# Norm steps given out beside products, TensorE's order fixed where the feed-forward begins

## The chip, the cores and the metric

The kernel runs on one core of a Trainium2 chip. The metric is the time of one execution on the device, in microseconds (us). Three runs of the kernel before gave 1806.92, 1814.36 and 1819.08 us; the median is 1814.36 us. The engines are named as the profile names them: PE is TensorE (matmul; PEld its weight load), DVE is VectorE, ACT is ScalarE, POOL is GpSimd, SP is SyncE, which issues most DMA transfers.

## The reference

One layer of a streaming encoder, for 1024 prompt frames and 32 sample frames of width 1024, in float32:

```python
h = h + (merged.astype(h.dtype) @ w_out).astype(h.dtype)      # merged: three gated branches
xn2 = rmsnorm(h, norm_ffn)                                     # y = h * rsqrt(mean(h*h) + 1e-6) * g
gu = xn2 @ w_gate_up                                           # 1024 -> 2 x 2816
gate, up = gu[..., :FFN_HIDDEN], gu[..., FFN_HIDDEN:]
h = h + ((jax.nn.silu(gate) * up) @ w_down).astype(h.dtype)    # 2816 -> 1024
y = rmsnorm(h, norm_final)
```

The mixers in front of `merged` (a state space model, spatial gating, stick-breaking attention) take about half of the time and are not touched.

## The kernel before

**Layout and products.** The rows of `h` lie in nine blocks: b = 0 to 7 are 128 prompt rows each, b = 8 the 32 sample rows. Half 0 is blocks 0 to 3, half 1 blocks 4 to 8. A float32 product is made of three matmuls (`mm3`, L144 to L146): each operand is split into a rounded high part (an ACT copy) and a remainder (a subtraction on DVE or POOL).

**The stages that matter.** `gates(half)` makes the merged branches `mt` (a high and a low tile, in eight slices m; for half 1 slice 3 is made last). `out_proj(half)` runs four quarters q of 256 columns; in each it multiplies `mt` of every block with a piece of `w_out` (24 matmuls of 128x256 a block, 16 of 64x256 for block 8) and DVE adds the result to `h`. `norm2(chunk)` then makes the operands of the feed-forward for one half. For each block it takes a sum of squares (ACT), the reciprocal root by bit trick and three Newton steps on one column (`rstd_of`, DVE), the scaled row tile `xb` (DVE), eight transposes of `xb` (PE, L1190), and from two pairs of blocks seven split operands each, by sums and differences of quarters (a Strassen-Winograd form: seven products in place of eight). `xb` has one buffer. `up_tile(i, chunks)` does one of the 22 tiles of 128 hidden columns: it loads two raw weight tiles, makes seven split stationary weights from them (L1244 to L1265: ACT, POOL and DVE), and runs seven products of 12 matmuls a chunk, in the order w1, w2, ws2, ws3, wu, ws1, ws4. Chunk 0 is 256 wide, chunk 1 is 272.

**The order of the program before** is: `gates(0)`, `out_proj(0)`, `gates(1)`, `norm2(0)`, `out_proj(1)`, `norm2(1)`, then a lead of tiles 0 and 1 with chunk 0 and tiles 0 and 1 with chunk 1 (weights are made anew for each of the four), then tiles 2 to 21 with both chunks. The down product reads the activations back from DRAM (`act_d`) in eleven groups of 256 rows (`load_act`: a DMA to `ra`, an ACT copy to `act`, remainders on POOL and DVE) and adds to `h`, which `norm2` stored in `h_d` and which comes back as `hd0` and `hd1`.

**What sets the order.** Every engine works its own instructions in order. A scheduler lays them out from the program's order, their dependencies and the buffers that are free; a DMA that SP issues waits behind the ones that stand before it. Large tiles share slots: pool `hx` and pool `hy` have four slots each, given out in turn; weights go through rings of four `wh`, four `wl` and two `raw` tiles; PSUM has six banks for products (`p`) and two for transposes (`ptn`).

Of the kernel before, what the change touches and what calls it, by code (L numbers as in the profile page):

```python
# [17 lines left out]
T = TP + TS  # L18
# [30 lines left out]
def trunk_kernel(ctx: ExitStack, tc: tile.TileContext,  # L49
# [1027 lines left out]

    def h_rows(b):
        return H[b // 4][:, b % 4, :] if b < 8 else hS


# [60 lines left out]
    def out_proj(half, mt):  # L1142
        wo = w_out[0].rearrange("(k p) c -> p k c", p=128)
        for q in range(4):
            us = tm_units(wo, 256 * q)
            for b, (t0, rows, h, off) in enumerate(BLOCKS):
                if h != half:
                    continue
                d = h_rows(b)[:, 256 * q:256 * q + 256]
                if b == 8:  # L1150
                    ps = ps_any()[0:64, 0:256]
                    tm_sample(ps, mt2, us)
                    tmp = late.tile([32, 512], F32, name="htmp")[:, 0:256]
                    add_pair(tmp, ps, tmp)
                    v.tensor_add(d, d, tmp)
                    continue
                ps = ps_any()[0:rows, 0:256]
                tm_dense(ps, mt, off, rows, us)
                v.tensor_add(d, ps, d)
# [4 lines left out]
    PAIRS = (((0, 2), (1, 3)), ((4, 6), (5, 7)))  # L1164
# [30 lines left out]

    def make_operands(wk, X, o, n, x11, x21, second):

        def split(i, raw, eng):
            hi, lo = X[i][0][:, :, o:o + n], X[i][1][:, :, o:o + n]
            s.activation(hi, raw, AF.Copy)  # L1200
            eng.tensor_sub(lo, raw, hi.bitcast(F32))

        def tmp(name, tag, bufs):
            return wk.tile([128, 4, 128], F32, name=name, tag=tag, bufs=bufs)[:, :, 0:n]

        r11 = tmp("r11", "r11", 1)
        s.activation(r11, x11, AF.Copy)
        split(0, x11, v)
        split(1, x21, v)
        x12, x22 = second()  # L1210
        t1 = tmp("t1", "xt", 2)
        v.tensor_sub(t1, x12, r11)
        split(3, t1, g)
        t2 = tmp("t2", "xt", 2)
        v.tensor_sub(t2, x22, t1)
        split(2, x22, v)
        split(4, t2, g)
        t3 = tmp("t3", "xt", 2)
        v.tensor_sub(t3, t2, r11)
        split(5, t3, g)  # L1220
        v.tensor_sub(r11, x21, t2)
        split(6, r11, g)

    def norm2(chunk, wk, X):
        for j, (ba, bb) in enumerate(PAIRS[chunk]):
            xa = scaled(wk, ba)
# [3 lines left out]
            def second():  # L1230
                xb = scaled(wk, bb)
                return [turned(xb, 128, q, ps_turn()) for q in range(2)]

            make_operands(wk, X, 128 * j, 128, x11, x21, second)
        if chunk:
            xs_ = scaled(wk, 8)
            a0, a1 = turned(xs_, 32, 0, ps_turn()), turned(xs_, 32, 1, ps_any())
            make_operands(wk, X, 256, 16, a0[:, :, 0:16], a1[:, :, 0:16], lambda: (a0[:, :, 16:32], a1[:, :, 16:32]))
        sp.dma_start(h_d[chunk], H[chunk])
# [12 lines left out]
    def up_tile(i, wk, chunks, X):  # L1252
# [12 lines left out]
        ws2, ws3, ws1, ws4 = stationary(g1, g), stationary(u1, v), stationary(u2, g), stationary(g2, g)  # L1265

        def product(w, x):
            out = {}
            for c in chunks:
                ps = out[c] = ps_any()[:, 0:WIDTH[c]]  # L1270
# [47 lines left out]
    with pool("wg", 1) as wk:  # L1318
        mA = gates(0, wk)
        sp.dma_start(gb, dram_bcast(norm_ffn, 1024))  # L1320
        out_proj(0, mA)
        mB = gates(1, wk)
    with pool("wu", 1) as wk:
# [3 lines left out]
        norm2(0, wk, X0)  # L1327
        out_proj(1, mB)
        sm = [big(hy, "xo4"), big(hy, "xo5"), big(hx, "xo6")]
# [124 lines left out]
```

## Time and profile before

| What | us |
|---|---|
| median of three runs | 1814.36 |
| the profiled execution, its own time | 1813.17 |
| its span, first to last instruction | 1811.5 |
| PE busy in the span | 1658.8 (92%) |
| DVE busy | 991.4 (55%) |
| ACT busy | 594.9 (33%) |
| POOL busy | 603.6 (33%) |
| chain that ended last: PE / DVE / issue / POOL | 61% / 15% / 10% / 6% |
| mean granted TensorE clock (1 is 2.4 GHz) | 0.954 |

How to read it: PE carries most of the chain, so time can be won where PE stands still or runs at the lower clock. In the profile's 40 slices PE's busy share falls to 5 tenths in slice 21, to 7 or 8 in its neighbours and again to 7 near slice 34; slices 21 and 23 to 25 are the stretch from the end of `gates(1)` to the first tiles of the feed-forward, and slice 34 is the hand-over to the down product.

### The profile page before, as it was taken

To read this page: it belongs to the slowest core of one execution; us is meant where nothing else is said; L and a number is where in the kernel's file an instruction comes from. 1 tells how busy PE (TensorE), PEld (TensorE's weight loads), DVE (VectorE), ACT (ScalarE), POOL (GpSimd) and SP (SyncE) were. 2 spreads that over 40 slices of the span, in tenths; PEclk is the share of its full clock that TensorE was granted. 3 is DMA by queue.
4 is the path that set the end of the run, shared out by engine and by line. 5 is a ranking of instruction groups with operands and counts; after the bars stand their busy time and mean duration, and the time that the engine had idled before them with its cause. 6 is when DMAs were issued, how large, how long until landed. Compare 5 with 4: busy or idle time off the path is not lost.

```text
span 1811.5 us, 28082 instructions
## 1 busy us (share of the span) xinstructions
PE 1658.8 (92%) x10949; PEld 1507.4 (83%) x10949; DVE 991.4 (55%) x1909; ACT 594.9 (33%) x1082; POOL 603.6 (33%) x363
## 2 busy tenths in 40 slices
PE   7988998999989899999978578999999997999997
PEld 6977896777777788799977578999999997888875
DVE  7952514312799730911285666666555554666645
ACT  5322322223566532212233333333333332212214
POOL 2210211333011233434444244333332334645534
PEclk9998999699999999999988889999999998999999
DMA  7453245256656427754351232322232225333202
GB/s 219 120 133 71 79 140 129 64 157 187 166 138 170 128 79 239 254 176 140 91 193 31 87 108 78 95 75 72 81 91 77 71 71 188 120 95 95 71 26 94
DMA packets 273502, 212.62 MB, mean 117 GB/s; under 512 B 68372, under 2 KB 246584, under 8 KB 272856
## 3 DMA queue, kind: packets, MB, share of 16 engines
q1 hardware_dynamic: 244808, 195.61, 36.7%
q10 hardware_dynamic: 28560, 15.21, 2.8%
q8 instruction: 86, 1.41, 0.3%
q14 instruction: 48, 0.39, 0.1%
HBM read 154.88 MB, written 55.30 MB: 116 GB/s over the span
## 4 chain that ended last, share of the span: by engine, by line
PE 61%; DVE 15%; issue 10%; POOL 6%; DMA 4%; ACT 3%; SPq 1%; POOLq 0%; ACTq 0%; DVEq 0%
PE p L146 13%; PE p L145 13%; PE p L144 13%; DVE om L831 4%; PE p_d L144 3%; PE p_d L146 3%; PE p_d L145 3%; POOL wl L118 3%; PE p_av L144 2%; PE p_av L146 1%; PE p_av L145 1%; DVE rs_m L169 1%; POOL hS L1401 1%; DMA raw<-in_w_gate_up_dram 1%; DVE wtl L862 1%
## 5 line engine op out<-in xcount | busy, mean ns | idle before, releaser
L118 POOL TENSOR_TENSOR wl<-raw,wh 128x1024 fp32r<-128x1024 f32 x120 | 303.1, 2533 | 760.7 <-ACT wh L117 702.9
L117 ACT ACTIVATE wh<-raw 128x1024 fp32r<-128x1024 f32 x120 | 126.4, 1058 | 360.4 <-PE p L146 160.0
L144 PE MATMUL p<-xo,wh 128*128 128x256 f32 (+1 forms) x616 | 177.1, 288 | 3.7 <-ACT wh L1248 1.8
L144 PE MATMUL p<-xo,wl 128*128 128x256 f32 (+1 forms) x616 | 176.9, 287 | 1.1 <-DVE fa L1305 1.1
L146 PE MATMUL p<-xo,wh 128*128 128x256 f32 (+1 forms) x616 | 177.0, 287 | 0.8 <-POOL wh L1249 0.8
L145 PE MATMUL p<-xo,wh 128*128 128x256 f32 (+1 forms) x616 | 177.5, 288 | 0.0
L146 PE MATMUL p<-xo,wl 128*128 128x256 f32 (+1 forms) x616 | 176.4, 286 | 0.9 <-POOL wl L1249 0.9
L145 PE MATMUL p<-xo,wl 128*128 128x256 f32 (+1 forms) x616 | 176.8, 287 | 0.0
L144 PE MATMUL p_d<-xnh,wh 128*128 128x272 f32 (+1 forms) x464 | 158.3, 341 | 10.4 <-ACT vb L377 7.2
L146 PE MATMUL p_d<-xnh,wl 128*128 128x272 f32 (+1 forms) x464 | 155.7, 336 | 5.2 <-POOL wl L118 5.2
L145 PE MATMUL p_d<-xnl,wh 128*128 128x272 f32 (+1 forms) x464 | 155.4, 335 | 0.0
L1407 DVE TENSOR_TENSOR hd<-p,hd 128x512 f32<-128x512 f32 x160 | 106.3, 683 | 65.7 <-PE p L146 65.7
L145 PE MATMUL p<-wl,act 128*128 128x512 f32 x352 | 138.6, 394 | 2.5 <-POOL wl L118 2.5
L146 PE MATMUL p<-wh,act 128*128 128x512 f32 x352 | 138.3, 393 | 0.0
L144 PE MATMUL p<-wh,act 128*128 128x512 f32 x352 | 138.0, 393 | 0.0
L1249 POOL TENSOR_TENSOR wh<-raw,wh 128x512 fp32r<-128x512 f32 x60 | 80.3, 1342 | 153.8 <-ACT wh L1248 153.8
L1249 POOL TENSOR_TENSOR wl<-raw,wl 128x512 fp32r<-128x512 f32 x60 | 79.9, 1334 | 154.4 <-ACT wl L1248 154.3
L144 PEld LDWEIGHTS p<-xo,wh 128*128 128x128 f32 x616 | 118.0, 192 | 4.1 <-ACT wh L1248 2.0
L144 PEld LDWEIGHTS p<-xo,wl 128*128 128x128 f32 x616 | 117.7, 191 | 2.0 <-issue 1.3
L146 PEld LDWEIGHTS p<-xo,wh 128*128 128x128 f32 x616 | 118.1, 192 | 1.1 <-POOL wh L1249 1.1
L146 PEld LDWEIGHTS p<-xo,wl 128*128 128x128 f32 x616 | 117.4, 191 | 1.4 <-POOL wl L1249 1.4
L145 PEld LDWEIGHTS p<-xo,wh 128*128 128x128 f32 x616 | 117.8, 191 | 0.0
(454 smaller groups left out, 4439.7 us busy)
## 6 DMA issues: line engine op xcount, KB each, us to landing
raw<-in_w_in_dram SPq DMA_DIRECT2D x66, 512.0 KB, 3.9
raw<-in_w_gate_up_dram SPq DMA_DIRECT2D x48, 512.0 KB, 4.6
ra<-act_d SPq DMA_DIRECT2D x22, 528.0 KB, 3.6
raw<-in_w_down_dram SPq DMA_DIRECT2D x22, 512.0 KB, 3.7
q<-q_d SPq DMA_DIRECT2D x64, 128.0 KB, 3.0
raw<-in_w_out_dram SPq DMA_DIRECT2D x16, 512.0 KB, 5.9
act_d<-fs SPq DMA_DIRECT2D x44, 128.0 KB, 4.0
act_d<-fa SPq DMA_DIRECT2D x44, 128.0 KB, 4.0
```

The lines of the kernel that those rows point to most:

```text
L117: s.activation(wh, raw, AF.Copy)
L118: g.tensor_sub(wl, raw, wh.bitcast(F32))
L144: pe.matmul(ps, ah, bh, start=start, stop=False)
L145: pe.matmul(ps, ah, bl, start=False, stop=False)
L146: pe.matmul(ps, al, bh, start=False, stop=stop)
L169: v.scalar_tensor_tensor(t, y, mh, y, op0=OP.mult, op1=OP.mult)
L831: v.tensor_tensor_scan(rev, rev, rev, 1.0, op0=OP.mult, op1=OP.bypass)
L862: v.tensor_sub(wl[:, lo:512], pt[:, lo:512], wh[:, lo:512].bitcast(F32))
L1249: eng.tensor_sub(lo, src, hi.bitcast(F32))
L1401: g.tensor_add(hr[:, cs], hr[:, cs], tmp)
L1407: v.tensor_add(hr[:, cs], ps, hr[:, cs])
```

## The change

Five things change, all between `out_proj(0)` and the first group of the down product.

1. The sums of squares move from `norm2` into `out_proj`: after the second and the fourth quarter ACT squares 512 columns of a block into a column of `ss2`. `norm2` adds the two and makes the reciprocal roots of all blocks of a half at once (`rstd_all`, 128x5).
2. The scaled rows `xb` are made by POOL (times the gain `gb`) and ACT (times the root) in place of one DVE instruction.
3. `norm2` becomes a generator. Its steps are given out beside products: `norm2(0)` beside `out_proj(1)` (transposes after every second block), `norm2(1)` beside tiles 0 and 1 of chunk 0 (transposes after every third product). PE's order in this stretch is taken as written (`manual_schedule`).
4. The lead is tile 0 and tile 1 with chunk 0, tile 1 with chunk 1 (its weights are held), tile 0 with chunk 1: three weight preparations in place of four. One remainder of the held tiles moves from DVE to POOL (`light`).
5. In the down product the first `act` takes a slot of `hx`, and `hd0`, `hd1` are allocated after it.

```diff
+    ss2 = late.tile([128, 20], F32, name="ss2")
...
-    def out_proj(half, mt):
+    def out_proj(half, mt, junk, beside=iter(())):
...
+            for b in PAIRS[half][0] + PAIRS[half][1] + ((8,) if half else ()):
+                t0, rows, h, off = BLOCKS[b]
+                next(beside, None)
...
+                if q % 2:
+                    c = slice(256 * q - 256, 256 * q + 256)
+                    s.activation(junk()[0:rows], h_rows(b)[:, c], AF.Square, scale=1.0 / 32,
+                                 accum_out=ss2[0:rows, 10 * half + 5 * (q // 2) + (b % 4 if b < 8 else 4):][:, 0:1])
...
-    def scaled(wk, b):
-        rows = BLOCKS[b][1]
-        xb = wk.tile([128, 1024], F32, name="xb")
-        hr = h_rows(b)
-        ss = wk.tile([128, 1], F32, name="rs_ss", bufs=2)
-        s.activation(xb[0:rows], hr, AF.Square, scale=1.0 / 32, accum_out=ss[0:rows])
-        r = rstd_of(wk, ss[0:rows], rows)
-        v.scalar_tensor_tensor(xb[0:rows], hr, r, gb[0:rows], op0=OP.mult, op1=OP.mult)
-        return xb[0:rows]
+    def rstd_all(wk, ss, n):
+
+        m = wk.tile([128, 20], F32, name="rs_a")
+        mm, y, t = [m[:, 5 * i:5 * i + n] for i in range(3)]
+        v.tensor_scalar(mm, ss, EPS, None, op0=OP.add)
+        v.tensor_scalar(y.bitcast(I32), mm.bitcast(I32), -0.5, 1597463007.0, op0=OP.mult, op1=OP.add)
+        v.tensor_scalar(mm, mm, -0.5, None, op0=OP.mult)
+        for _ in range(3):
+            v.tensor_mul(t, y, y)
+            v.tensor_mul(t, t, mm)
+            v.scalar_tensor_tensor(y, t, 1.5, y, op0=OP.add, op1=OP.mult)
+        return y
...
+    def norm2(chunk, wk, X, gap):
+
+        def scaled(b):
+            i, rows = b % 4 if b < 8 else 4, BLOCKS[b][1]
+            xb = wk.tile([128, 1024], F32, name="xb")[0:rows]
+            g.tensor_mul(xb, h_rows(b), gb[0:rows])
+            s.activation(xb, xb, AF.Copy, scale=r[0:rows, i:i + 1])
+            return xb
...
+        for j in range(2):
+            xa = scaled(order[2 * j])
+            for _ in range(gap):
+                yield
             x11 = turned(xa, 128, 0, ps_turn())
             x21 = turned(xa, 128, 1, ps_any())
...
-        norm2(0, wk, X0)
-        out_proj(1, mB)
...
-        norm2(1, wk, X1)
-        X = (X0, X1)
         NF = FF // 128
-        lead = 2
-        for c in range(2):
-            for i in range(lead):
-                up_tile(i, wk, (c,), X)
-        for i in range(lead, NF):
+        with tc.manual_schedule(engines={mybir.EngineType.PE}):
+            work = norm2(0, wk, X0, 2)
+            out_proj(1, mB, lambda: wk.tile([128, 512], F32, name="junk2", tag="xt", bufs=2), work)
+            for _ in work:
+                pass
...
+            work = norm2(1, wk, X1, 3)
+
+            up_tile(0, wk, (0,), X, up_weights(0, True), work)
+            held = up_weights(1, True)
+            up_tile(1, wk, (0,), X, held, work)
+            for _ in work:
+                pass
+        up_tile(1, wk, (1,), X, held)
+        up_tile(0, wk, (1,), X)
+        for i in range(2, NF):
             up_tile(i, wk, (0, 1), X)
...
-        for half in range(2):
-            H[half] = hx.tile([128, 4, 1024], F32, name=f"hd{half}", tag="hx")
-            sp.dma_start(H[half], h_d[half])
...
-        acts = [load_act(0), load_act(1)]
+        acts = [load_act(0, hx)]
+        for half in range(2):
+            H[half] = hx.tile([128, 4, 1024], F32, name=f"hd{half}", tag="hx")
+            sp.dma_start(H[half], h_d[half])
+        acts.append(load_act(1))
```

**How it moves instructions.** On PE, before the change, the end of `out_proj(1)` (L132 is block 8), all transposes of `norm2(1)` in a row, and the first product (of `xo`, the operands):

```order
L132 MATMUL p_9940<-wh,mt_6925 64x256
L132 MATMUL p_9940<-wl,mt_6925 64x256
L1190 MATMUL ptn<-ident,xb 128x128 x4
L1190 MATMUL p_9983<-ident,xb 128x128 x4
L1190 MATMUL ptn<-ident,xb 128x128 x12
L1190 MATMUL p_10054<-ident,xb 128x128 x4
L1190 MATMUL ptn<-ident,xb 128x128 x8
L1190 MATMUL ptn<-ident,xb 128x32 x4
L1190 MATMUL p_10125<-ident,xb 128x32 x4
L144 MATMUL p_10183<-xo_9266,wh 128x256
```

On PE with the change, the end of the third product of tile 0, chunk 0 (36 matmuls stand before this place since `out_proj(1)`), and the fourth product:

```order
L145 MATMUL p_10053<-xo_9286,wl 128x256
L146 MATMUL p_10053<-xo_9286,wl 128x256
L1202 MATMUL ptn<-ident,xb 128x128 x4
L1202 MATMUL p_10072<-ident,xb 128x128 x4
L144 MATMUL p_10086<-xo_9286,wh 128x256
L145 MATMUL p_10086<-xo_9286,wh 128x256
```

The transposes of each block now stand between products, and PE reaches them in this order whatever else is ready.

On POOL with the change, the piece from the scaling of the third block of half 1 (block 5) to that of block 8 (`xb` is the new product with the gain, `xo` an operand's remainder, `wh` and `wl` remainders of tile 1's weights):

```order
L1213 TENSOR_TENSOR xb<-h_9037,gb 128x1024
L1222 TENSOR_TENSOR xo_9973<-t_10142,xo_9973 128x4x128
L1222 TENSOR_TENSOR xo_9974<-t_10146,xo_9974 128x4x128
L1286 TENSOR_TENSOR wh<-raw,wh 128x512
L1286 TENSOR_TENSOR wl<-raw,wl 128x512
L1213 TENSOR_TENSOR xb<-h_9037,gb 128x1024
L1222 TENSOR_TENSOR xo_9974<-t_10152,xo_9974 128x4x128
L1222 TENSOR_TENSOR xo_9287<-r_10077,xo_9287 128x4x128
L1286 TENSOR_TENSOR wh<-raw,wh 128x512
L1286 TENSOR_TENSOR wl<-raw,wl 128x512
L1213 TENSOR_TENSOR xb<-hS,gb 32x1024
```

Before, POOL had no `xb` in its queue, and the eight large `xo` remainders of half 1 stood in two runs of four with one `wl` between them; now weights, remainders and scalings take turns.

On SP, the hand-over to the down product before the change (`hd0` is issued far ahead of this piece, right behind the weight loads of tile 1):

```order
L116 DMA raw<-in_w_down_dram 128x1024
L1347 DMA hd_15698<-h_d_6928 128x4096
L116 DMA raw<-in_w_down_dram 128x1024
L1313 DMA act_d<-fs 128x256 x2
L1316 DMA act_d<-fs 128x16
L116 DMA raw<-in_w_down_dram 128x1024
L1313 DMA act_d<-fa 128x256
L116 DMA raw<-in_w_down_dram 128x1024
L1313 DMA act_d<-fa 128x256
L1316 DMA act_d<-fa 128x16
L1355 DMA ra<-act_d 128x1056 x10
```

and with the change:

```order
L1355 DMA act_d<-fs 128x256 x2
L1358 DMA act_d<-fs 128x16
L116 DMA raw<-in_w_down_dram 128x1024
L1355 DMA act_d<-fa 128x256 x2
L1358 DMA act_d<-fa 128x16
L116 DMA raw<-in_w_down_dram 128x1024
L1401 DMA ra<-act_d 128x1056 x2
L1467 DMA hd_15650<-h_d_6929 128x4096
L1467 DMA hd_15652<-h_d_6930 128x4096
L1401 DMA ra<-act_d 128x1056 x6
```

The first two `ra` loads stand behind the last store to `act_d` in both; `hd0` and `hd1` have moved behind them.

## Rows read from the trace of the kernel before

**Rows 1.** Busy time by stretch (us): engines with instruction counts, granted clock, DMA share, GB/s.

```profile
935.76:962.17 26.41, 5.53 (x25) 4.76 (x25) 17.99 (x41) 9.66 (x17) 8.32 (x7) 0.55 0.13 40
962.17:1018.72 56.55, 56.55 (x466) 56.31 (x464) 26.48 (x55) 15.28 (x27) 19.77 (x12) 0.97 0.16 52
1018.72:1055.02 36.30, 6.81 (x33) 5.63 (x33) 25.52 (x56) 13.99 (x28) 13.37 (x11) 0.57 0.38 124
1055.02:1104.08 49.06, 45.48 (x338) 44.46 (x338) 31.88 (x55) 19.95 (x42) 22.12 (x19) 0.94 0.30 92
1521.79:1531.36 9.57, 0.01 (x2) 0.01 (x1) 2.53 (x3) 1.51 (x2) 2.54 (x2) 0.70 0.67 226
```

**Rows 2.** PE's waits from 935 to 1125 us: in total, times, longest.

```profile
PE ptn L1190 <- DVE xb L1184: 50.4, 7, 9.7
```

**Rows 3.** Instructions on the tile xb (ns, min/median/max).

```profile
L1184 DVE SCALAR_TENSOR_TENSOR xb<-h,rs_m,gb x8: 1283/1284/1287, 941.6 to 1041.9; 128x1024 f32<-128x1024 f32 x8
```

**Rows 4.** PE's timeline after the first gap: start, duration, line.

```profile
962.95 0.41 PE L144 MATMUL p<-wh,m 128*128 128x256 f32 x1
...
966.01 0.29 PE L144 MATMUL p<-wh,m 128*128 128x256 f32 x1
966.13 0.28 PE L145 MATMUL p<-wl,m 128*128 128x256 f32 x1
...
968.04 1.03 PE L1190 MATMUL ptn<-ident,xb 128*128 128x128 f32 x8
```

**Rows 5.** Timeline of ACT and DVE at the end of gates(1).

```profile
937.16 0.66 ACT L1132 ACTIVATE m<-acc 128x544 fp32r<-128x544 f32 x1 [0.38 <-DVE acc L1131]
...
937.85 2.07 DVE L1133 TENSOR_TENSOR m<-acc,m 128x544 fp32r<-128x544 f32 x1 [0.72 <-ACT m L1132]
```

**Rows 6.** Instructions on the tile xo (the operands), ns.

```profile
L1201 POOL TENSOR_TENSOR xo<-t,xo x15: 322/1270/1312, 952.4 to 1057.1; 128x512 fp32r<-128x512 f32 x12, 128x64 fp32r<-128x64 f32 x3
```

**Rows 7.** Instructions on yf, of line L1249, of line L118 and on hd, ns.

```profile
L1367 POOL TENSOR_TENSOR yf<-hd,gfin x8: 2347/2407/2411, 1759.3 to 1803.5; 128x1024 f32<-128x1024 f32 x8
L1370 ACT ACTIVATE yf<-yf,rs_m x8: 1132/1138/1153, 1764.0 to 1803.5; 128x1024 f32<-128x1024 f32 x7, 32x1024 f32<-32x1024 f32 x1
...
L1249 POOL TENSOR_TENSOR wl<-raw,wl x60: 1264/1294/1743, 1011.1 to 1499.0; 128x512 fp32r<-128x512 f32 x60
...
L118 POOL TENSOR_TENSOR wl<-raw,wh x120: 2339/2398/5723, 9.3 to 1751.3; 128x1024 fp32r<-128x1024 f32 x120
...
L1410 ACT ACTIVATE junk<-hd x16: 614/631/634, 1755.2 to 1804.5; 128x512 f32<-128x512 f32 x16
```

**Rows 8.** DVE's timeline in the root's Newton steps, and a remainder beside POOL.

```profile
957.02 1.19 DVE L170 SCALAR_TENSOR_TENSOR rs_m<-rs_m 128x1 f32<-128x1 f32 x1
...
958.50 0.16 DVE L170 SCALAR_TENSOR_TENSOR rs_m<-rs_m 128x1 f32<-128x1 f32 x1
...
1065.06 1.46 DVE L1249 TENSOR_TENSOR wl<-raw,wl 128x512 fp32r<-128x512 f32 x1
```

**Rows 9.** PE's timeline in tile 2: its waits in brackets.

```profile
1111.37 0.35 PE L144 MATMUL p<-xo,wl 128*128 128x256 f32 x1 [1.06 <-DVE fa L1305]
...
1120.76 0.39 PE L144 MATMUL p<-xo,wh 128*128 128x272 f32 x1 [1.83 <-DVE fs L1288]
```

**Rows 10.** Timeline at the hand-over to the down product.

```profile
1043.29 0.34 SPq L1347 DMA_DIRECT2D hd<-h_d  x1
...
1507.16 0.38 SPq L1347 DMA_DIRECT2D hd<-h_d  x1
...
1525.25 0.42 SPq L1316 DMA_DIRECT2D act_d<-fa  x1
1525.73 0.96 SPq L1355 DMA_DIRECT2D ra<-act_d  x2
1529.99 1.08 ACT L1356 ACTIVATE act<-ra 128x1056 fp32r<-128x1056 f32 x1 [7.26 <-DMA ra<-act_d]
...
1538.62 0.69 DVE L1407 TENSOR_TENSOR hd<-p,hd 128x512 f32<-128x512 f32 x1 [2.54 <-PE p L146]
```

More of the change, by code (lines that the diff above doesn't have):

```diff
@@ L1230, in second, with both @@
             def second():
-                xb = scaled(wk, bb)
+                xb = scaled(order[2 * j + 1])
+                for _ in range(gap):
+                    yield
                 return [turned(xb, 128, q, ps_turn()) for q in range(2)]
-            make_operands(wk, X, 128 * j, 128, x11, x21, second)
+            yield from operands_of(128 * j, 128, x11, x21, second)
         if chunk:
-            xs_ = scaled(wk, 8)
+            xs_ = scaled(8)
+            sp.dma_start(h_d[chunk], H[chunk])
+            for _ in range(gap):
+                yield
             a0, a1 = turned(xs_, 32, 0, ps_turn()), turned(xs_, 32, 1, ps_any())
-            make_operands(wk, X, 256, 16, a0[:, :, 0:16], a1[:, :, 0:16], lambda: (a0[:, :, 16:32], a1[:, :, 16:32]))
-        sp.dma_start(h_d[chunk], H[chunk])
+            def both():
+                yield
+                return a0[:, :, 16:32], a1[:, :, 16:32]
+            yield from operands_of(256, 16, a0[:, :, 0:16], a1[:, :, 0:16], both)
+        else:
+            sp.dma_start(h_d[chunk], H[chunk])
     wgu = w_gate_up[0].rearrange("(k p) c -> p k c", p=128)
@@ L1264, in up_tile @@
         v.tensor_sub(g2, g2, g1)
-        ws2, ws3, ws1, ws4 = stationary(g1, g), stationary(u1, v), stationary(u2, g), stationary(g2, g)
+        ws2, ws3, ws1, ws4 = stationary(g1, g), stationary(u1, g if light else v), stationary(u2, g), stationary(g2, g)
+        return w1, w2, ws2, ws3, wu, ws1, ws4
+    def up_tile(i, wk, chunks, X, weights=None, beside=iter(())):
+        w1, w2, ws2, ws3, wu, ws1, ws4 = weights or up_weights(i)
         def product(w, x):
@@ L1269, in product @@
             for c in chunks:
+                next(beside, None)
                 ps = out[c] = ps_any()[:, 0:WIDTH[c]]
@@ L1320, in trunk_kernel @@
         sp.dma_start(gb, dram_bcast(norm_ffn, 1024))
-        out_proj(0, mA)
+        out_proj(0, mA, lambda: wk.tile([128, 512], F32, name="junk2", tag="sgg", bufs=6))
         mB = gates(1, wk)
@@ L1344, in trunk_kernel, with load_act @@
         NG = FF // 256
-        for half in range(2):
-            H[half] = hx.tile([128, 4, 1024], F32, name=f"hd{half}", tag="hx")
-            sp.dma_start(H[half], h_d[half])
-        def load_act(gr):
-            act = hy.tile([128, 2, 2 * T], F32R, name="act", tag="hy")
+        def load_act(gr, p=hy):
+            act = p.tile([128, 2, 2 * T], F32R, name="act", tag="hx" if p is hx else "hy")
             for e in range(2):
@@ L1389, in down_groups @@
                 if last:
-                    ss = wk.tile([128, 2], F32, name="ss2")
+                    ss = wk.tile([128, 2], F32, name="ss3")
                 for n in range(2):
```

76 lines of the change are left out of this document (38 added, 38 removed).

## The prediction

> **What bounds the kernel now.** The page's first part says that PE is busy for 92% of the span, and the chain of waits gives it 61%, so I looked for where PE stands. The table of busy time by stretch [rows 1] is read next. In the 26.41 us after `gates(1)` PE works for 5.53 us at a granted clock of 0.55; in the 36.30 us after `out_proj(1)` for 6.81 us at 0.57; at the hand-over to the down product it does nothing for 9.57 us. The table of PE's waits [rows 2] names the first two: seven waits of transposes for `xb`, 50.4 us in all. DVE makes `xb` in 1.28 us [rows 3]; around that lie the square on ACT, the root and the one buffer of `xb`. The third thing to see is the restart: after the first gap matmuls start 0.2 us apart until about 966.0, then 0.12 us [rows 4]: the lower of the two clock levels, then the higher. Eighteen matmuls from 962.17 to 966.01 took 3.84 us where 18 x 0.12 = 2.16, so **one restart costs 1.7 us**. The lead of four single-chunk tiles takes 49.06 us [rows 1] and tile 2 waits another 1.06 + 1.83 us [rows 9].
>
> The sum is made against the profiled execution, 1813.17 us, which lies 1.2 us below the median of the three runs.
>
> **First stretch: `norm2(0)` beside `out_proj(1)`.** Before: 26.41 + 56.55 = 82.96 us [rows 1]. The second window holds one group of eight transposes, 1.03 us [rows 4], and one restart, so the products alone are 56.55 - 1.03 - 1.7 = 53.8 us. With the change:
> - products 53.8 us;
> - four groups of transposes, 4 x 1.03 = 4.1 us;
> - a wait that the old gap covered. `out_proj(1)` now follows `gates(1)` at once, and its first block can take slices 0 to 2 only (nine matmuls, 1.1 us, to 936.85). Slice 3's remainder leaves DVE at 937.85 + 2.07 = 939.92 [rows 5]. Less the two matmuls that need only the high part: 2.8 us, and a restart, 1.7 us;
> - one late `xb`, the third block's. Between the transposes of the second and third block PE has block 8 (16 matmuls) and one block (24), 40 x 0.12 = 4.8 us. In that time: POOL's product 2.41 us [rows 7], POOL's first remainder 1.27 us [rows 6], which frees a buffer for the next difference, two DVE subtractions at about 0.65 us (half of [rows 3], an estimate), an ACT copy of about 0.63 us (as the square of that size) and the scale 1.14 us [rows 7]: 6.8 us, with some 0.4 us of hand-overs 7.2 us, so 2.4 us late. The first, second and fourth find 5.8 us of products (two blocks) and need about 2.41 + 1.14 and three copies, so I cost them at nothing; without that cover they would be late by as much as the third.
>
> Sum 53.8 + 4.1 + 2.8 + 1.7 + 2.4 = 64.8 us. **Gain 18.2 us.** The squares moved into `out_proj` are 18 ACT instructions of at most 0.63 us [rows 7] on an engine with a third of the span busy; ACT waits there for each block's addition, and weight copies queue behind it, but they are made a quarter ahead. I cost them at nothing.
>
> **Second stretch: `norm2(1)` beside tiles 0 and 1.** Before: 36.30 + 49.06 + 2.89 = 88.25 us to where tile 2 runs free [rows 1, 9]. With the change, from the end of `out_proj(1)`:
> - (a) Three products (4.3 us), then the first transposes. Their `xb` needs the root, the root needs block 8's last square, and in ACT's order that stands behind the copy of product one: 2.9 us. Fourteen small DVE instructions at about 0.2 us (0.16 to 1.19 in [rows 8]) and two additions between them: 3.6 us. Scale 1.14, transposes 1.03: 8.7 us, and 0.8 us for small instructions that stand beside POOL's work as one in [rows 8] does: 9.5 us.
> - (b) Now POOL sets the pace. Until chunk 1 can begin it has four products with the gain at 2.41 us, eight remainders at 1.27, four small ones at 0.32, and seven weight remainders at 1.29 [rows 6, 7]: 9.6 + 10.2 + 1.3 + 9.0 = 30.1 us. PE has 11 products (15.8 us) and 3.6 us of transposes for the same time. POOL also waits about three times 2 us for transposes, a copy and a scale to come round (one buffer of `xb`): 6 us. Two us for DVE's sums beside POOL (1.46 in place of about 0.65 each, [rows 8]) and two for matmuls at the lower clock: 40 us.
> - (c) Chunk 1 of tiles 1 and 0: 168 matmuls of 272 columns at 0.12 x 272/256 = 0.1275 us, 21.4 us, and a restart: 23.1 us. Tile 1's weights are held, so one preparation (two loads, seven high and seven low parts) is gone, and tile 0's has the 10.7 us of tile 1 as cover; I take tile 2's 2.89 us of waits as gone too.
>
> Sum 72.6 us. **Gain 15.6 us.** Bounds of (b): 19.4 us, if PE's own work sets it, and 30.1 us x 5.72/2.40 = 72 us by the longest POOL instruction in [rows 7]; I take 40, since the medians there are tight.
>
> **The spare slot: nothing.** The first activations come late because `ra` is issued at 1525.73, right behind the last store at 1525.25, and ACT starts the copy into `act` when the data are there, at 1529.99 [rows 10]: the slot was not what it waited for. In SP's order with the change `ra` still stands behind that store. New is that `hd0` and `hd1`, issued at 1043.29 and 1507.16 before, now come right behind the first two `ra`. Those two (1.06 MB) took 4.3 us; 2.05 MB would by that take 8.2 us, so `hd0` lands about 12.5 us after 1525.73, at 1538.3, and its first reader was at 1538.62 [rows 10]. It just fits: 0, with 8.2 us as the other end.
>
> Total 18.2 + 15.6 = 33.8 us: **1779 us**.
>
> **Rivals.**
> 1. *All norm work is covered.* No late `xb`, the second stretch is PE's own: 168 x 0.12 + 4.6 + 21.4 = 46.2 us. Gain 20.6 + 42.0: 1751 us. For it: ACT and DVE have time. Against: POOL's 30.1 us in a stretch of 20 us of products. 13%.
> 2. *DVE is held up by POOL.* A small instruction takes 1.19 us beside POOL's work and 0.16 us without [rows 8], 1.03 us more. Some 23 DVE instructions of the second stretch (12 of the root, 11 on weights, operands and activations) lie beside POOL. All on the path: 24 us where 2.8 are in the sum, gain 12.6: 1801 us. Against: many have slack. 12%. The Trainium skill ("SBUF — State Buffer", Who interferes with whom) says that a DVE instruction with two SBUF inputs and a POOL one that reads SBUF share a read port, held for a whole instruction by whichever came first; it speaks against giving POOL the product with the gain, and by it the sum would end at this rival's time. The trace agrees in the rows cited, though not for each instruction.
> 3. *POOL becomes the bound and it is slower than before.* The same port may hold up POOL: its longest instruction of line L118 took 5.72 us against a median of 2.40 [rows 7]. Were the 30.1 us of (b) stretched so, they cost 41.8 us more: 1821 us. It decides from where POOL's instructions take 2.1 times as long (33.8 / 30.1 more). Against: the medians lie within 2% of the shortest. 5%.
> 4. *The spare slot does what it is for*: `ra` leaves before the last store and the 9.57 us go too: 1770 us. SP's order speaks against it. 5%.
>
> **The numbers.** The forecast, with 65%, has a range of its own from 1765 to 1795 (late `xb` and (b) within 15 us, `hd` up to 8 us). The range of 1753 to 1799 takes in rival 4, most of rival 2 and the forecast's tails; rival 1, rival 3 and a few per cent of rival 2 lie outside. A per cent (18 us) is about what a measurement here can tell from no change. Faster by more than that, below 1795 us: nearly all of the forecast, rivals 1 and 4, a third of rival 2: 85%. Within it: 10%. Slower: rival 3, 5%.
>
> **What would show it.** In the profile after, PE's waits for `xb` should fall from 50.4 us to under 25 us, with the releaser ACT, where they remain, and the longest in front of block 7's transposes; `out_proj(1)` should end 63 to 67 us after `gates(1)`; POOL should be busy for over 70% of the stretch of tiles 0 and 1 with chunk 0; a wait of 2 to 3 us for `m` should stand at the head of `out_proj(1)`; and the gap ahead of the down product should still be 9 to 11 us. The forecast is wrong if that stretch is as short as PE's products, or if POOL's instructions there take far more than their medians.

## The result, and the profile after

The changed kernel takes **1785.7 us** (median of four runs, 1782.7 to 1788.4) against 1813.3; the ratio is **0.985, with an interval of 0.981 to 0.989**. The forecast was 1779 us. The profiled execution took 1785.0 us, its span is 1783.3 us.

The table of busy time by stretch, of the kernel after, answers to [rows 1]. The lines are: `out_proj(1)` with `norm2(0)` beside it; from there to the first transposes of `norm2(1)`; from there to chunk 1; chunk 1 of tiles 1 and 0; the hand-over to the down product. Columns are as in [rows 1]: busy time of PE, weight loads, DVE, ACT and POOL, then the granted clock, the DMA share and GB/s.

```profile
932.69:999.22 66.53, 59.33 (x480) 58.52 (x480) 36.08 (x58) 28.90 (x52) 40.51 (x23) 0.95 0.16 52
999.22:1008.16 8.94, 5.38 (x47) 5.17 (x45) 4.58 (x17) 5.52 (x11) 4.01 (x3) 1.00 0.93 320
1008.16:1047.88 39.72, 24.59 (x166) 23.46 (x165) 26.44 (x37) 19.29 (x35) 29.93 (x19) 0.84 0.17 51
1047.88:1071.34 23.46, 23.46 (x171) 23.46 (x172) 11.52 (x24) 8.25 (x19) 9.44 (x10) 0.90 0.22 64
1487.30:1498.83 11.53, 0.00 (x1) 0.00 (x1) 3.33 (x4) 2.69 (x5) 2.55 (x2) 0.59 0.73 244
```

The first stretch went from 81.93 to 66.53 us. The 82.96 us of [rows 1] end at 1018.72, 1.03 us too late: eight transposes that stand in that window already belong to `norm2(1)`, and they begin where the matmuls of `out_proj(1)` end. PE's timeline before:

```profile
1017.57 0.28 PE L132 MATMUL p<-wl,mt 128*64 128x256 f32 x1
1017.69 0.60 PE L1190 MATMUL ptn<-ident,xb 128*128 128x128 f32 x4
```

In the third line of the table PE works for 24.59 of 39.72 us and POOL for 29.93, 75% of it. The last line is the gap ahead of the down product: it did not shrink, it grew from 9.57 to 11.53 us. (The profile before has PE's lowest slice, 5 tenths, as the 23rd of the 40, not the 21st.)

PE's waits from 933 to 1125 us, of the kernel after (total us, times, longest), answer to [rows 2] and [rows 9].

```profile
PE ptn L1202 <- ACT xb L1214: 12.1, 3, 4.5
PE p L144 <- ACT xo L1221: 6.3, 1, 6.3
PE p L144 <- DVE fs L1330: 3.3, 1, 3.3
PE p L144 <- ACT wh L1285: 2.1, 1, 2.1
PE p L146 <- POOL wh L1286: 1.6, 1, 1.6
PE p L146 <- DVE m L1139: 1.6, 1, 1.6
PE p L144 <- ACT m L1138: 1.0, 1, 1.0
...
```

The 50.4 us of waits for `xb` have become 12.1, with ACT as releaser. New are 6.3 us ahead of chunk 1 and 3.7 us for weights; tile 2's wait (`fs`) is still there with 3.3 us, where it was 1.06 + 1.83.

**Where 28.2 us of span went.** Cut at the end of `gates(1)`, at the end of `out_proj(1)`, at the end of the up product and at the first matmul of the down product, at the same points before and after (so at 1017.69 before): what lies ahead of the first cut 3.1 us shorter (the change touches `out_proj(0)` there, by its squares and by taking its blocks in pairs); the first stretch 15.4 shorter; from there to the end of the up product (504.10 to 488.08) 16.0 shorter; the hand-over 2.0 longer; the down product (280.14 to 284.47) 4.3 longer. The stages that the change can touch gained 25.1 us, against the forecast's 33.8. The experiments below ask four things: whether the cover is what gained, whether POOL paces the second stretch, what the spare slot does, and why the down product became slower.

### The profile page after: what moved, and what is told of

Same layout as the page of the kernel before. It is cut to its first block, busy times and chain, and to the rows that moved or that the text cites. A ratio compares the mean times of both kernels' runs of the same rounds, so it can differ in the third digit from the quotient of the medians.

```text
span 1783.3 us, 28031 instructions
## 1 busy us (share of the span) xinstructions
PE 1657.8 (93%) x10949; PEld 1502.6 (84%) x10949; DVE 964.7 (54%) x1838; ACT 603.6 (34%) x1102; POOL 623.3 (35%) x369
## 5 line engine op out<-in xcount | busy, mean ns | idle before, releaser
L118 POOL TENSOR_TENSOR wl<-raw,wh 128x1024 fp32r<-128x1024 f32 x120 | 304.6, 2544 | 747.1 <-ACT wh L117 705.9
L144 PE MATMUL p_d<-xnh,wh 128*128 128x272 f32 (+1 forms) x464 | 157.9, 340 | 10.4 <-ACT vb L377 7.2
L1286 POOL TENSOR_TENSOR wh<-raw,wh 128x512 fp32r<-128x512 f32 x59 | 77.6, 1317 | 147.1 <-ACT wh L1285 142.7
L1286 POOL TENSOR_TENSOR wl<-raw,wl 128x512 fp32r<-128x512 f32 x58 | 78.4, 1353 | 141.4 <-ACT wl L1285 141.4
```

The lines of the kernel that those rows point to most:

```text
L118: g.tensor_sub(wl, raw, wh.bitcast(F32))
L144: pe.matmul(ps, ah, bh, start=start, stop=False)
L1286: eng.tensor_sub(lo, src, hi.bitcast(F32))
```

## Experiments

Times of one kernel differ by up to 20 us between executions (the kernel before: 1797 to 1820). Profiles differ most ahead of the end of `gates(1)` (last section), so I compare stages of the profiles beside the ratios to the kernel before (each with its 95% interval). The stages, in us: A from the end of `gates(1)` to the end of the up product, B the hand-over, C the down product.

| kernel | A | B | C | A+B+C | ratio |
|---|---|---|---|---|---|
| before | 586.0 | 9.6 | 280.1 | 875.7 | 1 |
| changed kernel | 554.6 | 11.5 | 284.5 | 850.6 | 0.985 (0.981 to 0.989) |
| changed kernel again | 553.7 | 11.3 | 284.6 | 849.6 | 0.984 (0.980 to 0.988) |
| only `norm2(0)` beside | 559.3 | 11.4 | 284.6 | 855.3 | 0.987 (0.983 to 0.991) |
| only `norm2(1)` beside | 571.1 | 11.6 | 284.1 | 866.7 | 0.995 (0.992 to 0.999) |
| hand-over as before | 552.7 | 11.5 | 285.1 | 849.2 | 0.986 (0.982 to 0.990) |
| `xb` by DVE | 550.2 | 11.2 | 283.4 | 844.8 | 0.978 (0.975 to 0.980) |
| block 8 first | 553.3 | 11.4 | 284.5 | 849.2 | 0.982 (0.978 to 0.986) |
| before, `hy` shifted by 96 bytes | 584.0 | 10.1 | 286.0 | 880.1 | 0.999 (0.996 to 1.002) |
| `ss2` of 128 bytes | 555.1 | 11.6 | 284.7 | 851.5 | 0.983 (0.981 to 0.985) |
| `ss2` behind `h` | 558.8 | 11.2 | 278.2 | 848.2 | 0.981 (0.976 to 0.985) |
| early activations | 561.3 | -0.2 | 291.9 | 853.0 | 0.982 (0.979 to 0.984) |
| the same, small remainders on POOL | 556.7 | -0.2 | 286.2 | 842.7 | 0.980 (0.975 to 0.984) |
| the three best together | 555.7 | -0.2 | 277.6 | 833.1 | **0.974 (0.969 to 0.978)** |

**The changed kernel once more.**

> The changed kernel once more, as the measure of what varies from one execution to the next. Theory A (the slower down product belongs to the new places of its tiles): the matmuls of the down product start 0.234 us apart again, as in the first profile of it (0.228 before the change), and the part from the first to the last instruction of the down product takes 284 to 285 us. Theory B (it belongs to the one execution): the spacing comes out anywhere between 0.228 and 0.234. Time 1783 to 1789 us by both; out_proj(1) ends 65 to 66 us after gates(1), and the gap ahead of the down product is 11 to 12 us.

1781.6 us. The stages repeat within 1 us, and so does the spacing of the down product's matmuls (0.234 us). The slower down product belongs to the kernel, not to the execution.

**Each norm alone beside products.** Each kernel runs one of the two generators to its end at once:

```
             work = norm2(1, wk, X1, 3)
+            for _ in work:
+                pass
```

and the other one the same two lines behind `work = norm2(0, wk, X0, 2)`.

> norm2(1) is run through before tile 0 begins, so that only norm2(0) stands beside products. Theory (cover): the first stretch keeps its 17.5 us, PE's waits for xb after out_proj(1) come back (about 5 + 4 + 9 + 4 + 9 = 31 us), and of the second stretch's 13 us only what the held weights and the added POOL remainder give stays, about 4: 1793 to 1799 us. Rival (the hand-written order and the held weights give the gain, not the cover): within 3 us of the changed kernel, 1783 to 1789 us.

> norm2(0) is run through before out_proj(1) begins, so that only norm2(1) stands beside products. Theory (the two gains add): the first stretch goes back to about 82 to 85 us, since a block without cover costs POOL's 2.4 us and ACT's 1.15 us where DVE took 1.28 and the root is made once; the second stretch as in the changed kernel: 1801 to 1807 us. Rival (the gains overlap, because ACT and POOL get a backlog in out_proj(1) that they work off in the second stretch): less than 12 us lost, under 1798 us.

1787.3 and 1800.0 us, where the changed kernel has 1781.6 on the same chip. So losing the cover of `norm2(1)` costs 5.7 us, and losing that of `norm2(0)` 18.4. PE's waits for `xb` in the uncovered part show it, of `norm2(1)` (first fence) and of `norm2(0)` (second):

```profile
PE ptn L1202 <- ACT xb L1214: 22.7, 5, 7.4
...
```

```profile
PE ptn L1202 <- ACT xb L1214: 21.2, 4, 9.9
...
```

For `norm2(0)` the theory holds: the first stretch is back at 84.0 us, so all of its gain is cover (the time, 1800.0, lies 1 us under the theory's range). For `norm2(1)` neither theory does: 1787.3 us lies in the rival's range, but the loss is 5.7 us and not under 3. SP issues tile 3's last store at (before, the repeat of the changed kernel, `norm2(1)` uncovered)

```profile
1156.91 0.42 SPq L1316 DMA_DIRECT2D act_d<-fa  x1
```

```profile
1121.27 0.42 SPq L1358 DMA_DIRECT2D act_d<-fa  x1
```

```profile
1125.84 0.43 SPq L1358 DMA_DIRECT2D act_d<-fa  x1
```

From the end of `out_proj(1)` that is 139.2 us before, 123.4 in the repeat of the changed kernel and 128.8 uncovered: of a gain of 15.8 us **only 5.4 are cover, and 10.4 stay without it**. The uncovered norm waits 22.7 us for `xb` where the old one waited 29.5 of the 50.4 in [rows 2]. In the code there is one root in place of five, and POOL's product can start before a block's operands are done; no run shows which of the two shortens the waits. The rest, some 3.6 us, must lie in the lead of four tiles (held weights, one more weight remainder on POOL); I didn't part these.

**POOL as the pace of the second stretch: `xb` by DVE.**

```
-            g.tensor_mul(xb, h_rows(b), gb[0:rows])
-            s.activation(xb, xb, AF.Copy, scale=r[0:rows, i:i + 1])
+            v.scalar_tensor_tensor(xb, h_rows(b), r[0:rows, i:i + 1], gb[0:rows], op0=OP.mult, op1=OP.mult)
```

> The changed kernel, but each xb is made by one DVE instruction (1.28 us in the kernel before) where POOL's product with the gain (2.4 us) and ACT's scale (1.15 us) make it now. Theory A (POOL sets the pace of tiles 0 and 1 with chunk 0, as the prediction had it): four products fewer are 9.6 us fewer on POOL, the stretch from the first transposes of norm2(1) to chunk 1 falls from 39.7 to 30 to 33 us, the late third xb of the first stretch (4.5 us) goes too: 8 to 14 us less than the changed kernel, 1772 to 1778 us. Theory B (the stretch is a chain of hand-overs through single buffers, and POOL is only one member of it): each of the nine blocks comes 2.3 us earlier, but only those that PE waits for count: 2 to 6 us less. Theory C (DVE beside POOL is held up, so that work moved onto DVE is paid for there): no gain or a loss, 1784 us or more.

1776.2 us, and stage A is 3.5 to 4.4 us shorter than in the two profiles of the changed kernel. That is theory B's size. The time lies in theory A's range too, but the stretch that A named, from the first transposes of `norm2(1)` to chunk 1, is 35.4 us, where A asked for 30 to 33. POOL is busy for 22.70 us there in place of 29.93, 7.2 us less and not 9.6, which brought 4.3 us; the first stretch (66.3 us) gained nothing. PE's longest waits in 940 to 1060 us of this kernel are now

```profile
PE p L144 <- ACT wh L1284: 4.8, 1, 4.8
PE p L144 <- ACT xo L1220: 4.6, 1, 4.6
PE ptn L1202 <- DVE xb L1213: 4.4, 2, 3.6
PE ptn L1202 <- DVE xo L1221: 3.3, 1, 3.3
...
```

So of the 12.1 us of waits for `xb` 7.7 are gone. In the first stretch PE waits 3.3 us for DVE's remainder `xo` in place of 4.5 for `xb`, and in the second 4.8 us for tile 1's weights in place of 2.1.

**Another order of the same work: block 8 first in `norm2(1)`.** The block that stood behind the loop over the pairs is moved ahead of it.

> The changed kernel with block 8 taken first in norm2(1) in place of last. At the head of chunk 1 PE waits 6.3 us for the first operand of block 8's 16 columns, which ACT makes only when POOL is through with the last remainder of block 7 (one buffer). Theory A (a chain through that buffer, not POOL's amount of work, ends this stretch): the wait before chunk 1 falls to under 2 us, since the operands that block 7 makes last are needed two products later, and the head of the stretch loses at most 2: 3 to 5 us less than the changed kernel. Theory B (POOL's work sets the pace of the whole stretch, as the prediction had it): the same work in another order takes the same time, within 2 us.

1776.9 us (on another chip), and stage A changed by 0.4 to 1.3 us: theory B's answer. PE's waits of 932 to 1060 us:

```profile
PE ptn L1202 <- ACT xb L1214: 11.5, 3, 5.6
PE p L144 <- ACT xo L1221: 4.4, 1, 4.4
...
```

The wait ahead of chunk 1 fell from 6.3 to 4.4 us, and the first wait for `xb` rose from 3.6 to 5.6. Block 8's transposes now stand inside chunk 1, which takes 27.9 us to tile 2 in place of 23.2. The buffer was the last link there, not the bound. Taken with the run before it, neither POOL's work alone nor this one chain sets the pace; the ring of POOL, ACT, DVE and PE hands on about as much as it gains, and which link is the dearest stays open.

**The hand-over as it was** (`hd0` and `hd1` loaded ahead of the first activations, all of `act` in `hy`):

```
-        acts = [load_act(0, hx)]
         for half in range(2):
             ...
-        acts.append(load_act(1))
+        acts = [load_act(0), load_act(1)]
```

> The changed kernel with the hand-over to the down product as it was: hd0 and hd1 are loaded first, early in the up product as their slots come free, and all activations go into hy. Theory A (the new hand-over costs): the gap ahead of the down product falls from 11.5 to about 9.6 us, the matmuls of the down product start 0.228 us apart in place of 0.234, and the time falls by 2 to 6 us to 1780 to 1784 us. Theory B (both differences are of the one execution): 1784 to 1788 us, within 2 us of the changed kernel on the same chip, with a spacing that does not go with the change.

1783.8 us where the changed kernel has 1781.6 on the same chip, and a gap of 11.45 us: no difference. The spare slot is worth nothing, as forecast, and it is not to blame for the longer gap either. With it undone the down product was as slow, with 0.234 us from its first group on. In the changed kernel the first group's matmuls, whose `act` lies in `hx`, start 0.227 us apart and those of the later groups, with `act` in `hy`, 0.234. Two pieces of PE's timeline of the changed kernel show it, one from the first group and one from a later one, each from a matmul to the 21st behind it (4.76 and 4.92 us):

```profile
1510.23 0.39 PE L144 MATMUL p<-wh,act 128*128 128x512 f32 x1
...
1514.99 0.39 PE L144 MATMUL p<-wh,act 128*128 128x512 f32 x1
```

```profile
1569.80 0.39 PE L145 MATMUL p<-wl,act 128*128 128x512 f32 x1
...
1574.72 0.39 PE L145 MATMUL p<-wl,act 128*128 128x512 f32 x1
```

This pointed to the place of `act`: the new tile `ss2` (20 floats, 96 bytes of each partition with its rounding) stands ahead of `hy` and moves all of its tiles.

**Three runs on the place of `act`.** `ss2` of 128 bytes; the kernel before with an unused tile of 96 bytes; `ss2` behind the rows of `h`:

```
-    ss2 = late.tile([128, 20], F32, name="ss2")
+    ss2 = late.tile([128, 32], F32, name="ss2")
```

```
+    shift = late.tile([128, 20], F32, name="shift")
+    v.memset(shift, 0.5)
```

```
-        H[half] = hx.tile([128, 4, 1024], F32, name=f"h{half}", tag="hx")
+        ht = hx.tile([128, 4096 + 10], F32, name=f"h{half}", tag="hx")
+        H[half] = ht[:, 0:4096].rearrange("p (b c) -> p b c", c=1024)
+        SS[half] = ht[:, 4096:4106]
```

> The changed kernel with the new tile ss2 made 32 floats wide in place of 20, so that it takes 128 bytes of each partition in place of 96, and the tiles behind it (act among them, in hy) begin at multiples of 64 bytes again, as before the change. In the five profiles so far that have ss2 at 96 bytes, the matmuls of the down product start 0.234 us apart, except those of the first group where its act lies in hx, which start 0.227 us apart, as all do in the kernel before. Theory A (it is the place of act): 0.227 us throughout, and the down product takes 280 us in place of 284.5: 4 us less than the changed kernel, 1778 to 1783 us. Theory B (it is something else in the changed kernel): 0.234 us again, and the same time as the changed kernel.

> The kernel before the change with one unused tile of 96 bytes of each partition in the same pool, which moves hy's tiles by as much and does nothing else. Theory A (the place of act sets the spacing): the matmuls of the down product start 0.234 us apart, its part takes 284 to 285 us, and the kernel is 4 us slower than before, ratio 1.001 to 1.004. Theory B (something else): 0.227 us, ratio 1.000, and a down product of 280 us.

> The changed kernel with the sums of squares (the tile ss2) put behind the rows of h in its own slot of hx, where 1024 bytes of each partition are free, so that every tile of hy stands where it stood before the change. With ss2 of 96 or of 128 bytes ahead of hy, the matmuls whose act lies in hy start 0.234 and 0.233 us apart, those whose act lies in hx 0.227; the kernel before with a shift of 96 bytes also has 0.234 and a down product that is 5.8 us longer. Theory A (the place of act, by more than 64 bytes' alignment): 0.227 us throughout, the down product from 284.5 to about 280 us, 3 to 6 us less than the changed kernel, ratio to the kernel before 0.980 to 0.983. Theory B (128 bytes would have been enough, so the place is not what counts): 0.233 us again and no gain.

One line of the table of busy time by stretch for each kernel: 100 us from the middle of the down product, PE busy throughout at the full clock; the number of matmuls in them is what differs. In turn the kernel before, before with the shift, the changed kernel, `ss2` of 128 bytes, `ss2` behind `h`:

```profile
1591.50:1691.50 100.00, 100.00 (x442) 80.91 (x441) 64.06 (x86) 20.13 (x24) 52.04 (x27) 1.00 0.31 96
```

```profile
1592.30:1692.30 100.00, 100.00 (x429) 78.82 (x428) 61.96 (x83) 20.11 (x24) 47.91 (x24) 1.00 0.28 88
```

```profile
1563.30:1663.30 100.00, 100.00 (x429) 78.82 (x428) 61.95 (x83) 20.11 (x24) 48.13 (x25) 1.00 0.29 91
```

```profile
1562.50:1662.50 100.00, 100.00 (x432) 79.41 (x432) 61.98 (x83) 20.11 (x24) 48.15 (x25) 1.00 0.30 91
```

```profile
1547.40:1647.40 100.00, 100.00 (x442) 80.98 (x441) 64.69 (x87) 20.36 (x25) 53.54 (x27) 1.00 0.32 96
```

**An unused tile of 96 bytes makes the kernel before do 429 matmuls where it did 442, and its down product goes from 280.1 to 286.0 us; the old places give the changed kernel its 442 and 278.2 us back.** My guess that 64 bytes would do was wrong (0.232 us on the mean with 128 bytes). The whole times show little of it: 0.999 for the shifted kernel, and A+B+C of `ss2` behind `h` only 1.4 to 2.4 us less, since stage A is 4 to 5 us longer there. Of that, 2.7 us come from the up product, whose operands `xo` lie in `hy` too and gain by the shift what `act` loses: tiles 4 to 21 follow each other every 20.67 us in the two kernels with the old places (before, and `ss2` behind `h`), every 20.53 us in all eleven with the 96 bytes, the kernel before with the shift among them, and every 20.51 with 128 bytes. 380 us from the middle of the up product, full clock throughout, of the kernel before and of the same with the shift:

```profile
1135.00:1515.00 380.00, 380.00 (x3091) 380.00 (x3090) 225.36 (x441) 119.96 (x242) 122.47 (x92) 1.00 0.28 84
```

```profile
1130.00:1510.00 380.00, 380.00 (x3111) 380.00 (x3110) 223.45 (x441) 120.64 (x242) 123.17 (x92) 1.00 0.29 86
```

Another 2 us lie in the first stretch, which took 66.4 to 68.8 us in kernels whose edits do not touch it; why is open.

**The first activations early.** The function that loads them is moved ahead of the up product, and

```
             up_tile(i, wk, (0, 1), X)
+            if i == 4:
+                acts = [load_act(0, wk, hx)]
```

> The spare slot used in earnest: the activations of the down product's first group (rows that tiles 0 and 1 stored long before) are loaded and split into the free slot of hx beside tile 5, so that the down product can begin at once; hd0 and hd1 are loaded as their slots come free. Theory (the gap is the way of the first activations: the last store, the load, ACT's copy): the gap of 11.4 us falls to under 2 us, and matmuls at the lower clock behind it go as well: 10 to 13 us less than the changed kernel, 1772 to 1776 us. Rival (another thing is late there, the weights of the first group or hd): PE waits for that in turn, 0 to 5 us gained, 1780 to 1786 us.

1782.7 us. The gap is gone, PE goes from the up product into the down product without a stop, and most of it is lost again: C is 7.4 us longer, A about 7. The timeline of this kernel some 35 us into the down product:

```profile
1520.29 5.32 DVE L1374 TENSOR_TENSOR act<-ra,act 128x32 fp32r<-128x32 f32 x1
...
1520.91 4.64 POOL L1373 TENSOR_TENSOR act<-ra,act 128x1024 fp32r<-128x1024 f32 x2
...
1525.53 0.67 DVE L136 TENSOR_TENSOR htmp<-p,htmp 32x512 f32<-32x512 f32 x1
...
1526.25 0.57 PE L144 MATMUL p<-wh,act 128*128 128x512 f32 x1 [4.17 <-DVE htmp L136]
```

A remainder of 32 columns, 0.17 us at its shortest in this kernel, stands on DVE until POOL is through with two of 2.4 us; the evictions of PSUM behind it wait, and PE with them.

**The same with the small remainder on POOL** (`v.tensor_sub(act[:, e, T:T + TS], ...)` becomes `g.tensor_sub`, nothing else).

> As the kernel with the first activations loaded beside tile 5, with one more change: the small remainder of each activation (128x32) goes to POOL, behind its large one, and no longer to DVE. In the run before, the gap ahead of the down product was gone, but PE then waited 0.9 + 2.5 + 4.2 us for DVE's additions to hd, which stood behind small remainders of 5.0 and 5.3 us (0.18 us when POOL is idle); the profile of the changed kernel has them at 0.2 to 2.5 us. Theory A (DVE is held up by POOL's work and what is queued behind it waits): those three waits go, the down product falls from 291.9 to about 284.5 us, 10 to 12 us less than the changed kernel, ratio 0.977 to 0.980. Theory B (DVE stood still for the loads or for the weights, not for POOL): the waits stay under another name, less than 6 us gained.

1771.3 us. C is 286.2, 5.7 us less than in the run before it (the 4.6 us less in stage A can't come from this edit; 2.3 of them lie in the first stretch), and A+B+C is 842.7, 7 to 8 less than the changed kernel. Of PE's two kinds of wait for DVE (4.2 us for `htmp`, 3.6 for `hd` in the run before it) one is left:

```profile
PE p L144 <- DVE htmp L136: 3.0, 1, 3.0
```

Theory A, with 7 to 8 us in place of 10 to 12: this one wait stays, and stage A is 2 to 3 us longer; tile 3, which takes 23.3 us there in place of 20.5, is the larger part of it.

**Together: a faster version.** `xb` by DVE, the early activations with small remainders on POOL, and `act` in `hy` put 160 bytes further on in its slot:

```
+        at = 0 if p is hx else 40
+        act = p.tile([128, 4 * T + at], F32R, name="act", tag="hx" if p is hx else "hy")
+        act = act[:, at:].rearrange("p (e c) -> p e c", c=2 * T)
```

> Three things together on the changed kernel: each xb by one DVE instruction, the first activations loaded beside tile 5 with all remainders of the activations on POOL, and in hy every act 160 bytes further on in its slot, so that it begins at 128 modulo 256 bytes, as in the kernel before, while the operands xo of the up product stay where the change put them (with them there its matmuls ran at 8.24 a microsecond, at the old places at 8.14 to 8.18). The stages from the end of gates(1) on took 850.6 us in the changed kernel, 842.7 with the early activations and small remainders on POOL, 844.8 with xb by DVE. Theory A (the three add, and it is the place modulo 256 bytes that sets the pace of the down product): its matmuls start 0.227 us apart throughout, the stages take about 832 to 834 us, 17 us less than the changed kernel, ratio to the kernel before 0.974 to 0.978. Theory B (the place counts by another measure than modulo 256 bytes): 0.233 us from the second group on, and 838 to 840 us. Theory C (the parts get in each other's way, DVE with xb above all): 843 us or more.

**1767.6 us, ratio 0.974 (0.969 to 0.978)**; A+B+C is 833.1 us, inside the 832 to 834 of theory A, and the down product runs as in the kernel before:

```profile
1560.00:1660.00 100.00, 100.00 (x442) 80.47 (x441) 50.21 (x76) 24.30 (x29) 52.67 (x34) 1.00 0.27 86
```

## Why the prediction was right, and where not

**First stretch: 64.8 us against 66.5, and one reading wrong.** The sum takes one group of eight transposes out of the window before, which holds two (the second from 1017.69 us on, shown with the result). Read so, the products are 52.8 us, the sum is 63.8, and the 66.5 measured lie 2.7 us above it. The wait at the head of `out_proj(1)` was sized at 2.8 us and is 1.05 + 1.60. Only the third `xb` is clearly late, as forecast, but by 4.5 us, not 2.4, which is 2.1 of the 2.7. The timeline of the kernel after shows the step that failed:

```profile
950.57 2.41 POOL L1213 TENSOR_TENSOR xb<-h,gb 128x1024 f32<-128x1024 f32 x1 [4.09 <-PE ptn L1202]
...
954.18 2.35 POOL L118 TENSOR_TENSOR wl<-raw,wh 128x1024 fp32r<-128x1024 f32 x1
954.26 2.83 DVE L1240 TENSOR_TENSOR t<-t,r 128x512 f32<-128x512 f32 x1 [2.75 <-POOL xo L1222]
...
957.12 0.63 ACT L1221 ACTIVATE xo<-t 128x512 fp32r<-128x512 f32 x1 [3.78 <-DVE t L1240]
...
958.38 1.13 ACT L1214 ACTIVATE xb<-xb,rs_a 128x1024 f32<-128x1024 f32 x1
```

I counted DVE's subtraction at 0.65 us. It took 2.83, because POOL was in a weight's remainder that I had not put there, and the scale of the finished `xb` stood behind a copy that waited for it.

**Second stretch: the sum was right for reasons that are only half right.** Step (a) 9.5 us, measured 8.94; (b) 40, measured 39.7; (c) 23.1, measured 23.5. That tile 2's waits go was wrong: 2.8 to 3.3 us for `fs` in its two profiles, and tile 2 takes 25.5 to 25.9 us where it took 24.8. What made up for it was in no term: the place of `xo`, 2.7 us in tiles 3 to 21. And (b) was told as POOL's pace, but 7.2 us less on POOL gave 4.3, so that 40 came out as 39.7 is in part luck. And the gain was told as cover, when 10.4 of 15.8 us stay without cover.

**Rival 2 is at work, at a price below its own.** DVE's groups in 999.22 to 1047.88 us of the kernel after (total busy us, mean ns of one):

```profile
L1240 DVE TENSOR_TENSOR t<-t,r 128x512 f32<-128x512 f32 x2 | 2.9, 1446 | 2.4 <-POOL xo L1222 2.4
L1298 DVE TENSOR_TENSOR raw<-raw 128x512 f32<-128x512 f32 x1 | 2.9, 2890 | 0.0
L1352 DVE TENSOR_TENSOR fa<-fa,fu 128x256 f32<-128x256 f32 x2 | 2.8, 1386 | 0.5 <-ACT fa L1351 0.5
...
L1343 DVE TENSOR_TENSOR fs<-fs,ft 128x256 f32<-128x256 f32 x2 | 1.9, 966 | 0.0
L1236 DVE TENSOR_TENSOR t<-ptn,t 128x512 f32<-128x512 f32 x2 | 1.4, 686 | 0.1
...
L1190 DVE TENSOR_SCALAR rs_a<-ss 128x5 f32<-128x5 f32 x1 | 1.2, 1224 | 0.0
...
L1334 DVE TENSOR_TENSOR fa<-p,fa 128x256 f32<-128x256 f32 x2 | 0.8, 422 | 0.1
```

The first three lines, with both inputs in SBUF, take two to four times as long as those of their size that read one input from PSUM (`p`, `ptn`): 1.5 + 2.2 + 1.9 = 5.6 us more. The four others with two SBUF inputs (L1343, and behind the dots L1286 with 1370 ns, L1301 with 1168 and L1300 with 1117) take 1.6 to 2.3 times as long, 2.7 us more: 8.3 us in all, where (b) allowed 2 and rival 2 asked for 24. How much of the 8.3 us PE had to wait for, no run shows. The Trainium skill ("SBUF — State Buffer", Who interferes with whom) says just this of DVE's second SBUF input and POOL's reads; the trace agrees, and the rule explains which instructions are hit, which I had not used to choose between them. One line is hit without a second SBUF input: the `TENSOR_SCALAR` on 128x5 took 1.22 us beside a remainder on POOL and 0.18 us in the first stretch. Moving the 32-column remainder to POOL, with no other change, took 5.7 us off the down product.

**The spare slot: 0, as forecast**, shown by undoing it. Rival 4 asked what it would be worth if it worked: with the activations in place early the gap is 0, and after its own losses 7 to 8 us remain. The gap's 2.0 us more, against the 9 to 11 that I named, read off the timeline after: the last store is issued 4.3 us after PE's end (3.5 before), a weight load stands between it and `ra` (SP's order with the change, printed ahead of the prediction, has it there), and the data take 4.8 us to ACT's start where they took 4.3.

```profile
1491.61 0.43 SPq L1358 DMA_DIRECT2D act_d<-fa  x1
1492.13 0.40 SPq L116 DMA_DIRECT2D raw<-in_w_down_dram  x1
1492.62 0.86 SPq L1401 DMA_DIRECT2D ra<-act_d  x2
...
1497.46 1.08 ACT L1402 ACTIVATE act<-ra 128x1056 fp32r<-128x1056 f32 x1 [8.64 <-DMA ra<-act_d]
```

**What was missing** is a step that no view of the kernel before could show: the new tile moves `act`, and the down product is 4.3 us longer; it moves `xo` as well, which gave 2.7 us back in the up product. Cut at 1017.69 before, the forecast's gains are 17.1 and 16.7 us. With 1.7 us missing from the first stretch, 0.7 from the second (the 2.7 us counted in) and 2.0 of the hand-over, the 4.3 us make the 8.7 us by which the stages missed the forecast; an execution that was 3.1 us quicker ahead of the end of `gates(1)` hides a part of it.

Of the signs named: 12.1 us of waits for `xb` (under 25), 66.5 us to the end of `out_proj(1)` (63 to 67), POOL 75% busy (over 70) and 2.65 us for `m` (2 to 3) came as told. The longest wait for `xb` stood in front of the third block of `norm2(0)` (4.5 us), with block 7 second (4.0).

## What to carry to other kernels

Before calling a gain "cover", run the moved work uncovered: here two thirds of the second norm's gain came without it. Ask of each DVE instruction that will run beside POOL where its inputs lie, and keep those with two SBUF inputs, however small, out of the queue of PSUM evictions. And when a small new tile goes into a pool, compare the spacing of matmuls in stages that the change does not touch: here one stage gained 2.7 us by 96 bytes and another lost 4.3.

## What the runs showed of the hardware that I had not expected

- **The spacing of matmuls depends on where the stationary operand lies in a partition.** By the addresses in the built programs, `act` in `hy` begins at 128, 224 or 0 modulo 256 bytes (before; `ss2` of 96 bytes; of 128 bytes), and the spacing is 0.227, 0.234 and 0.232 us at the full clock. In `hx` it begins at 128, with 0.227. At 128 modulo 256 by another way, in the last kernel, it is 0.227 again; there `act` begins at 384 modulo 1024 where before it was 128, so 256 is enough of a measure for these four places. Why, and whether other remainders are better still, stays open.
- **The place of the moving operand counts too, and the other way round.** Of what PE reads in the up product only `xo`, the moving operand, lies in `hy`. Where `hy` begins at 128, 224 and 0 modulo 256 bytes, a tile takes 20.67, 20.53 and 20.51 us, and matmuls of 272 columns start on the mean 0.1261, 0.1249 and 0.1252 us apart. The place that costs the down product time gains some here.
- **Small DVE work can be stretched by far more than its size.** A subtraction of 128x32 took 0.17 to 5.32 us in one kernel; in the 5.32 us POOL worked for 4.64 beside it.
- **One stretch ahead of the change has two outcomes.** In 312 to 356 us the granted clock was 0.63 in the repeat of the changed kernel (first line) and 0.92 with `ss2` behind `h` (second). The program is the same there. With two clock levels, of which 0.5 is the lower, TensorE spent most of the 44 us at the lower one in the first and at the higher one in the second; three of the fourteen profiles have the second outcome, and `gates(1)` ends at 918 to 923 us in those and at 930 to 940 in the others. The difference, 10 to 20 us, is as large as what executions of one kernel differ by; but no kernel was profiled in both outcomes, so that this is the reason is not shown.

```profile
312.00:356.00 44.00, 40.67 (x133) 30.43 (x134) 14.25 (x13) 8.36 (x12) 12.41 (x6) 0.63 0.21 64
```

```profile
312.00:356.00 44.00, 39.81 (x183) 30.74 (x184) 23.84 (x15) 10.51 (x16) 22.00 (x7) 0.92 0.30 90
```
